# Another order of the first norm and the token mixer, and an output projection that ends with the prompt's tile and picks the prompt's tokens by one-hot products

## The chip, the cores and the metric

The program runs on one core of one Trainium2 chip. The metric is the device time of one execution in microseconds (us); lower is better. A core has five instruction queues that run beside each other, each strictly in its own order: TensorE (PE) for products, VectorE (DVE), ScalarE (ACT) and GpSimd (POOL) for elementwise work, and SyncE (SP), which here issues nearly all loads and stores. An instruction starts when it is first in its queue and what it waits for on the other engines has come.

## The reference, cut to what matters

One layer is computed for a prompt of 128 tokens (context) and 1024 latent tokens, with model width 1024: a modulated norm, a token mixer, a gated residual, a second modulated norm, and 16 experts that choose their tokens.

```python
mod = silu(c) @ w_mod + b_mod                    # 6 rows of 1024, once for the prompt, once for the latents
hn  = rmsnorm(x, norm1) * (1 + scale1) + shift1
u   = hn @ w_in                                  # p (512), v (1024), g1 and g2 (1024 each)
v   = conv4(v);  r, i = sigmoid(v @ w_r), sigmoid(v @ w_i)
a   = exp(-8 * r * softplus(-lam));  h_t = a h + sqrt(1 - a*a) * i * v      # scanned both ways
merged = sigmoid(g1) * (pool(p) @ w_br_pool) + sigmoid(g2) * (y_lru @ w_br_lru)
x  = x + gate1 * (merged @ w_out)
hn = rmsnorm(x, norm2) * (1 + scale2) + shift2
aff = softmax(hn @ router_w);  gate, idx = top_k(aff per expert, 2 * n / 16)   # 16 prompt, 128 latent tokens
out = (silu(hn[idx] @ w1) * (hn[idx] @ w3)) @ w2 * gate                        # for each of 16 experts
x  = x + gate2 * scatter_add(out);  y = rmsnorm(x, final)
```

## The kernel before

The 1152 tokens lie in tiles of 128: tile 0 is the prompt, tiles 1 to 8 the latents. A product in near fp32 precision is made of three passes: each weight block is loaded as `raw`, ScalarE rounds it to `hi` (L188), VectorE takes the rest as `lo` (L189), and PE adds hi·x_hi, hi·x_lo and lo·x_hi (L198 to L200). `do_split(n)` issues loads and splits for all entries of a list of work, `seq`, below n; it runs some four entries ahead of the products. There are three `raw` buffers, each free again once its `lo` is made.

The stages follow each other: the first norm with the modulation rows it needs (entries `a`; chunks in `DP` go through PE unsplit) to about 85 us; the mixer to about 565 us; the branch projection (L757) to about 665 us; the output projection (L984 to L986, two halves of 512 columns a tile, in the order of `steps`) to 803.3 us; a transition to the first expert product (L1465) at 832.6 us; then 16 experts of some 79 us each.

In the mixer each entry of `seq` is a block of 128 output channels: `v`, `g2`, `g1`, `p`, `bp`. Between them stand entries `m`, each eight products for a part of the remaining modulation rows (L665, L666). For each block j of v, `gates(j)` makes four groups of products and four Sigmoids on ScalarE (L527), `gates_rest(j)` is a row of Tanh, Exp, Square and Sqrt on ScalarE (L537 to L547) alternating with VectorE (L543 to L548), and `scans(j)` is VectorE's scan and what follows it (L559 to L568). [...] At ("g1", 0) the code runs `scans(6)`, `gates(7)`, then the splits of the next entries, and leaves `gates_rest(7)` in the list `rests` until the next `m` is done; then ("g2", 7) follows.

In the projection `project(i, h)` multiplies the sum by the gate row (`tmp`, L980) and adds it to the tile's x (L981), both on VectorE. `norm2` of a finished tile stores x (`x3_d`) and hn (`hn_d`, for the prompt `hp_d`) from SP. The router's products, the softmax (`affinities`), and the ranks among the latents (`first_rank`, `part_ranks`, a comparison with a transposed row) are hung into later steps; `prompt_a`, `prompt_b`, `prompt_c` choose the prompt's 16 tokens for each expert. Tile 8 comes last, so its norm, router and rank stand in the transition, followed by the latent list (`list_make`), an indirect gather of the first expert's rows from `hn_d` on POOL's queue (L1315), transposes of what it brought (L1446), and the first expert. `gate2_to` gives out 16 products of the last modulation row (L1299) in between, on w_mod blocks loaded into `hi` tiles by SP (L1292). Experts' weights come in 1 MB chunks (L1268).

Of the kernel before, what the change touches and what calls it, by code (L numbers as in the profile page):

```python
# [49 lines left out]
def hybrid_step_kernel(ctx: ExitStack, tc: tile.TileContext, x_prompt, x_sample, state_lru, c, c_ctx,  # L50
# [23 lines left out]
    hp_d = dram.tile([SP, D], F32, name="hp_d")  # L74
# [46 lines left out]
    l_a = ini.tile([P, 16], F32, name="l_a")  # L121
    l_e = ini.tile([P, 16], F32, name="l_e")
    l_z = ini.tile([P, 16], F32, name="l_z")
    l_q = ini.tile([P, 16], F32, name="l_q")
# [105 lines left out]
    for n, jb in enumerate(seq[4:]):  # L230
        full.append(jb)
        if n < 32 - 2 * NGT:
            full.append(("m", n))
# [118 lines left out]
    def hn_cols(k):  # L352
        for x, z in ((xv[:, k, 0, :SP], 0), (xv[:, k, 0, SP:], 1), (xv[:, k, 1:], 1)):
            V.tensor_scalar(x, x, s1[:, z, k:k + 1], modc[:, 0, z, k:k + 1], op0=OP.mult, op1=OP.add)
        A.copy(hn_hi[:, k, :].rearrange("p (g t) -> p g t", g=3), xv[:, k])
# [88 lines left out]
    hn_first(0)  # L444
    do_split(8)

    for q in range(4):
        k = 2 * q
        if q < 3:
            do_split(4 * q + 10)  # L450
# [3 lines left out]
        hn_cols(k + 1)  # L454
# [4 lines left out]
        if q < 3:  # L459
            mod_low(q + 1)  # L460
            do_split(4 * q + 12 if q < 2 else HEAD + 2)
# [6 lines left out]
    softplus()  # L468
# [19 lines left out]
    LR = {}  # L488

# [119 lines left out]
    def pool_evac(g, a3):  # L609
# [95 lines left out]
    rests = []  # L705
    load_gates(0)
    v_evac(va[0])
    conv(0)
    for j in range(2):
# [12 lines left out]
    for i in range(HEAD + 2, len(seq)):  # L722
        kind, j = seq[i]
        if kind == "m" and (kind, j) not in spl and i < done_split[0]:
            continue
        if (kind, j) != ("g1", 0):
            do_split(i + 4)
        for d in list(later):
            d[0] -= 1
            if d[0] <= 0:  # L730
                d[1]()
                later.remove(d)
        if kind == "bl" and j == 0:
            mg_hi = pool_sb["dp"].tile([P, KD, T], F32R, name="mg_hi", tag="D")
            mg_lo = big.tile([P, KD, T], F32R, name="mg_lo", tag="H2")
        if kind == "m":
            mod_block(j // 2, j % 2, spl.pop((kind, j)))
            for f in rests:
                f()
            rests = []  # L740
# [137 lines left out]
    g1r, mrows = [wo_g[:, KD * D:(KD + 1) * D].bitcast(F32), wop.tile([P, D], F32, name="g1r1")], {}  # L878
    for z in range(2):
        G.dma_start(g1r[z], row(z))  # L880
    x2s = {}
    for i in (1, 2):
        x2s[i] = sgp.tile([P, T], F32, name="sg")[:, :D]
        G.dma_start(x2s[i], x_rows(i))
# [9 lines left out]
    pgi = route.tile([P, 2], I32, name="pgi")  # L894
# [44 lines left out]
    def load_mrows(z):  # L939
        mrows[z] = [tk.tile([P, D], F32, name=f"s2r{z}", bufs=1),  # L940
                    tk.tile([P, D], F32, name="t2r", bufs=1) if z else rk.tile([P, D], F32, name="t2r0", tag="arow")]
        for n in range(2):
            SY.dma_start(mrows[z][n], row(2 + 2 * n + z))

    SY.dma_start(x2p, x_rows(0))
    load_mrows(1)
    load_mrows(0)

    def last_rows():
        x2s[8] = tk.tile([P, D], F32, name="x2l", tag="s2r0", bufs=1)  # L950
        SY.dma_start(x2s[8], x_rows(8))
# [3 lines left out]
    def project(i, h, mid=(), part=False):  # L955
        z = 1 if i else 0
        hs = slice(h * 512, (h + 1) * 512)
        if h == 0 and i not in x2s:
            x2s[i] = x2p if i == 0 else sgp.tile([P, T], F32, name="sg")[:, :D]
            if i:  # L960
                SY.dma_start(x2s[i], x_rows(i))
# [19 lines left out]
        V.tensor_tensor(x2s[i][:, hs], x2s[i][:, hs], tmp, op=OP.add)  # L981
# [12 lines left out]
    def norm2_b(i, n=1):  # L994
        z = 1 if i else 0
        x2, hn = x2s[i], hns[i]
        for q in range(n):
            s = slice(q * D // n, (q + 1) * D // n)
            V.scalar_tensor_tensor(hn[:, s], x2[:, s], rs2[:, i:i + 1], mrows[z][0][:, s], op0=OP.mult, op1=OP.mult)
            V.tensor_tensor(hn[:, s], hn[:, s], mrows[z][1][:, s], op=OP.add)  # L1000
        if z:
            SY.dma_start(x3_d[(i - 1) * P:i * P, :], x2)
        SY.dma_start(hn_d[(i - 1) * P:i * P, :] if i else hp_d[:, :], hn)
# [6 lines left out]
    def router_a(i):  # L1010
        hts[i] = tk.tile([P, KD, P], F32, name="ht", bufs=1)
        for h in range(2):
            t = tp_tile()
            for k in range(4):
                PE.transpose(t[:, k * P:(k + 1) * P], x2s[i][:, (4 * h + k) * P:(4 * h + k + 1) * P], ident)
            A.copy(hts[i][:, 4 * h:4 * h + 4, :], t.rearrange("p (a b) -> p a b", a=4))

    def router_b(i):
        z = 1 if i else 0
        t = tp_tile()  # L1020
        for k in range(KD):
            PE.matmul(t[:, :E], hts[i][:, k, :], rws[:, z, k, :], start=k == 0, stop=k == KD - 1)
        lts[i] = t
# [71 lines left out]
    def last_rank():  # L1095

        beat = first_rank(7, 0, 8, 1)
        t = tp_tile()
        for i in range(7):
            PE.matmul(t[:, i:i + 1], beat[:, i * P:(i + 1) * P], ones[:, 0:1], start=True, stop=True)  # L1100
        V.tensor_reduce(rank, wins, axis=AX.X, op=OP.add)
        V.tensor_tensor(rank[:, :7], rank[:, :7], t[:, :7], op=OP.subtract)

# [84 lines left out]
    def prompt_c():  # L1188
# [7 lines left out]
        V.tensor_copy(pgi, pgf)  # L1196
# [6 lines left out]
    steps = [(1, 0), (0, 0), (1, 1), (0, 1)] + [(i, h) for i in range(2, NT) for h in range(2)]  # L1203

    pre, mids, post = ([[] for _ in steps] for _ in range(3))
    n = 4
    for i in [1, 0] + list(range(2, NT - 1)):
        n = max(n + 1, 2 * i + 2)
        a, b = (4, KD - 1)
        mids[n].append((a, lambda i=i: router_a(i)))  # L1210
        mids[n].append((b, lambda i=i: (router_b(i), router_c(i))))
    pre[2].append(constants)
    pre[8].append(last_rows)
    pre[2].append(router_weights)
    mids[4].append((KD - 1, router_shift))
# [581 lines left out]
```

## Time and profile before

| | us |
|---|---|
| median of 3 runs | 2151.72 (2150.81 to 2152.35) |
| profiled execution | 2155.95 |
| its span, first to last instruction | 2154.2 |
| PE busy in the span | 2070.4 (96%) |
| DVE, ACT, POOL busy | 1709.6, 1358.8, 190.9 |

The span is what the trace covers; 1.75 us of the profiled execution lie around it. An engine's busy time says how full it was over all stages; what a change is worth in one stage is read from what PE waits for there. The granted clock of PE is 0.983 in the mean: in a few stretches it is half.

### The profile page before, as it was taken

Reading aid. Unit: us, or ns where it says so; the run is one execution under the profiler, and the core shown is the slowest. Engines: PE = TensorE matmul, PEld = TensorE weight load, DVE = VectorE, ACT = ScalarE, POOL = GpSimd, SP = SyncE. Lnnn points to the kernel's source line nnn. Section 1 sums busy time; section 2 is a strip of 40 time slices with the busy share of each in tenths; the row PEclk is TensorE's granted clock in tenths of the full one; section 3 lists DMA queues with packets and bytes.
Section 4 is the critical chain, followed back from the end, with each engine's and each line's share of the span. In section 5 each row is a group of like instructions: output and inputs, shape, how many; then the busy total and the mean of one; then the engine's idle time right before and its main releaser. Section 6 shows DMA issues by size and latency. Waiting matters only on the chain.

```text
span 2154.2 us, 40533 instructions
## 1 busy us (share of the span) xinstructions
PE 2070.4 (96%) x17269; PEld 1974.4 (92%) x17269; DVE 1709.6 (79%) x1847; ACT 1358.8 (63%) x1444; POOL 190.9 (9%) x324
## 2 busy tenths in 40 slices
PE   6999999999999987899999999999999999999995
PEld 4799998999998875899999999999999999999994
DVE  6788988732236467988988898998998998899896
ACT  6477675321112225677877777877877777777783
POOL 0000001010101001020010010011010011011021
PEclk9999999999999988999999999999999999999997
DMA  8133434174644238699999999999999999999995
GB/s 265 56 118 114 125 111 124 55 223 117 203 158 170 109 110 296 237 326 332 346 328 334 343 331 324 343 340 326 333 335 327 338 341 328 336 341 323 339 313 181
DMA packets 304820, 543.91 MB, mean 252 GB/s; under 512 B 16300, under 2 KB 85628, under 8 KB 304639
## 3 DMA queue, kind: packets, MB, share of 16 engines
q1 hardware_dynamic: 285306, 478.56, 64.0%
q0 software_dynamic: 15728, 52.77, 8.4%
q10 hardware_dynamic: 3604, 9.98, 1.4%
q8 instruction: 135, 2.21, 0.4%
q14 instruction: 47, 0.38, 0.1%
HBM read 500.60 MB, written 40.67 MB: 251 GB/s over the span
## 4 chain that ended last, share of the span: by engine, by line
PE 86%; DVE 8%; DMA 2%; ACT 2%; issue 1%; SPq 0%; DVEq 0%; ACTq 0%
PE ac L1465 37%; PE ac L1473 17%; PE a L198 6%; PE a L199 6%; PE a L200 6%; PE a L757 5%; DVE lo L1280 2%; PE a L984 1%; PE a L986 1%; PE a L985 1%; DMA xg<-hn_d,lgi 1%; PE tp L1404 1%; PE tp L1489 1%; DVE lo L189 1%; PE tp L665 1%
## 5 line engine op out<-in xcount | busy, mean ns | idle before, releaser
L1280 DVE TENSOR_TENSOR lo<-raw,hi 128x2048 bf16<-128x2048 f32 x384 | 870.9, 2281 | 0.0
L1274 ACT CAST hi<-raw 128x2048 fp32r<-128x2048 f32 x384 | 729.4, 1912 | 3.8 <-issue 2.2
L1465 PE MATMUL ac<-x,hi 128*128 128x288 f32 x4096 | 606.1, 300 | 0.0
L1465 PEld LDWEIGHTS ac<-x,hi 128*128 128x128 f32 x4096 | 553.0, 189 | 1.0 <-issue 0.9
L1473 PEld LDWEIGHTS <-lo 128*128 128x128 bf16 x6144 | 380.4, 98 | 36.7 <-DVE lo L1280 0.8
L1465 PE MATMUL ac<-hh,hi 128*128 128x288 f32 x2048 | 332.9, 304 | 0.0
L1478 ACT COPY bs<-ac 128x288 f32<-128x288 f32 x320 | 127.8, 399 | 290.6 <-PE ac L1473 289.1
L1473 PE MATMUL ac<-xb,lo 128*128 128x144 bf16 x4096 | 302.4, 227 | 0.6 <-DVE lo L1280 0.6
L1465 PEld LDWEIGHTS ac<-hh,hi 128*128 128x128 f32 x2048 | 279.9, 189 | 0.0
L198 PE MATMUL a<-hn_hi,hi 128*128 128x384 f32 x624 | 212.0, 340 | 0.0
L199 PE MATMUL a<-hn_lo,hi 128*128 128x384 f32 x624 | 210.8, 338 | 0.0
L200 PE MATMUL a<-hn_hi,lo 128*128 128x384 f32 x624 | 210.8, 338 | 0.0
L1473 PE MATMUL ac<-hb,lo 128*128 128x144 bf16 x2048 | 171.9, 227 | 0.0
L189 DVE TENSOR_TENSOR lo<-raw,hi 128x1024 fp32r<-128x1024 f32 (+1 forms) x76 | 86.7, 1163 | 78.8 <-ACT hi L188 78.2
L1479 DVE TENSOR_TENSOR h<-ac,bs 128x288 f32<-128x288 f32 x256 | 115.7, 452 | 42.1 <-ACT bs L1478 41.8
L198 PEld LDWEIGHTS a<-hn_hi,hi 128*128 128x128 f32 x624 | 117.1, 188 | 0.4
L199 PEld LDWEIGHTS a<-hn_lo,hi 128*128 128x128 f32 x624 | 117.2, 188 | 0.0
L200 PEld LDWEIGHTS a<-hn_hi,lo 128*128 128x128 f32 x624 | 117.2, 188 | 0.0
L1710 POOL TENSOR_TENSOR yps<-ot,modc 128x128 f32<-128x128 f32 x16 | 35.9, 2247 | 735.2 <-DVE ot L1479 735.2
L188 ACT CAST hi<-raw 128x1024 fp32r<-128x1024 f32 (+1 forms) x76 | 74.8, 1001 | 41.2 <-PE a L199 33.3
L1479 DVE TENSOR_TENSOR ot<-ac,bs 128x288 f32<-128x288 f32 x64 | 29.3, 457 | 69.7 <-ACT bs L1478 69.7
L699 ACT ACTIVATE sg<-a 128x1152 f32<-128x1152 f32 x16 | 18.1, 1134 | 82.4 <-PE a L200 82.3
(447 smaller groups left out, 2626.8 us busy)
## 6 DMA issues: line engine op xcount, KB each, us to landing
raw<-in_exp_w_dram SPq DMA_DIRECT2D x380, 1024.0 KB, 7.2
raw<-in_w_in_dram SPq DMA_DIRECT2D x28, 512.0 KB, 5.0
raw<-in_w_mod_dram SPq DMA_DIRECT2D x28, 512.0 KB, 5.3
araw<-in_w_mod_dram SPq DMA_DIRECT2D x18, 256.0 KB, 4.5
g_d<-sg ACTq DMA_DIRECT2D x8, 576.0 KB, 3.2
yh_d<-yh POOLq DMA_DIRECT2D x8, 576.0 KB, 3.1
yl_d<-yl POOLq DMA_DIRECT2D x8, 576.0 KB, 4.6
m_d<-sg POOLq DMA_DIRECT2D x8, 576.0 KB, 4.2
```

Source lines behind the costliest of these rows:

```text
L188: A.copy(h, raw)
L189: V.tensor_tensor(l, raw, h.bitcast(F32), op=OP.subtract)
L198: PE.matmul(out, whi, xhi, start=first, stop=False)
L199: PE.matmul(out, whi, xlo, start=False, stop=False)
L200: PE.matmul(out, wlo, xhi, start=False, stop=last)
L757: PE.matmul(a3[:, ch, :CH], w[:, k, :], y[:, k, cs], start=n == 0 and k == 0 and w is hi, stop=n == 1 and k == KD - 1 and w is ws[-1])
L1274: A.copy(hl[n][0], raw[n])
L1280: V.tensor_tensor(lo, r, hi.bitcast(F32), op=OP.subtract)
L1465: PE.matmul(a[:, r, :2 * S], w[0][:, k, c0 + r * P:c0 + (r + 1) * P], x2(kk), start=kk == first, stop=False)
L1473: PE.matmul(a[:, r, S:2 * S], w[1][:, k, c0 + r * P:c0 + (r + 1) * P], xb(kk), start=False, stop=kk == last)
L1478: A.copy(b, a[:, :, S:2 * S])
L1479: V.tensor_tensor(dst, a[:, :, :S], b, op=OP.add)
```

## The change

Seven things are altered, in two regions.

First norm and mixer. Three chunks of modulation weights instead of four go unsplit. Some splits of the head stand earlier, `hn_cols` is cut in its VectorE part (`hn_mod`, now ahead of the splits' `lo`) and its ScalarE part, the copy of `mrow1` is one instruction of ScalarE, and the 21 small instructions of `softplus` stand behind `conv(0)`. In `seq`, four `m` follow ("g1", 0) instead of one, and fewer stand later. A new function `sums_next(n)` runs the next n entries `m`: one behind each `v_evac` and inside each `pool_evac`, four at ("g1", 0) between `scans(6)` and `gates(7)`. `gates_rest(7)` is issued at once, behind `gates(7)`.

Projection and transition. The latents come first and tile 0 last, so that norm, router and rank of tile 8 run under tile 0's products. The addition into x of tiles 1 to 7 goes to POOL. The prompt's choice comes after the loop. The two gathers of prompt rows from `hp_d` go; in their place `prompt_pick` builds a one-hot matrix (scaled by the norm), and `prompt_cols` multiplies x of the prompt by it, eight products of 128x128 for each half of the experts, and applies scale and shift as it copies. `gate2_to` gives eight products in the transition and eight behind the first group of expert 0 (only the last two of four column blocks are made here). All five first expert chunks are issued by SP, two ahead of the w_mod blocks; ScalarE issued four (chunks 2 to 5) before.

```diff
-DP = range(4)
+DP = range(3)
...
     for jb in seq[4:]:
         full.append(jb)
-        if n < 32 - 2 * NGT:
-            full.append(("m", n))
+        for _ in range(4 if jb == ("g1", 0) else 1):
+            if n < 32 - 2 * NGT:
+                full.append(("m", n))
+                n += 1
...
+            hn_mod(k + 1)
+        do_split(4 * q + 10 if q < 3 else HEAD + 2)
         dense_v(0, k)
...
-        hn_cols(k + 1)
+        hn_high(k + 1)
         dense_v(1, k)
...
+    def sums_next(n):
+
+        while n and seq[at[0] + 1][0] == "m":
+            at[0] += 1
+            m = seq[at[0]][1]
+            do_split(at[0] + 1)
+            turn_later()
+            mod_block(m // 2, m % 2, spl.pop(("m", m)))
...
             if j == 0:
                 g1s[j] = gate_evac(a3)
                 scans(KD - 2)
+                sums_next(4)
                 gates(KD - 1)
                 do_split(i + 5)
-                rests.append(lambda: gates_rest(KD - 1))
+                gates_rest(KD - 1)
...
-        V.tensor_tensor(x2s[i][:, hs], x2s[i][:, hs], tmp, op=OP.add)
+        (G if 0 < i < NT - 1 else V).tensor_tensor(x2s[i][:, hs], x2s[i][:, hs], tmp, op=OP.add)
...
-    steps = [(1, 0), (0, 0), (1, 1), (0, 1)] + [(i, h) for i in range(2, NT) for h in range(2)]
+    steps = [(1, 0), (2, 0), (1, 1), (2, 1)] + [(i, h) for i in list(range(3, NT)) + [0] for h in range(2)]
...
-    load_chunk(0)
+    for n in range(2):
+        load_chunk(n)
     for j in range(4 - NGT, 4):
-        if j == 5 - NGT:
-            SY.dma_start(x3_d[7 * P:, :], x2s[8])
         gate2.append(ew.tile([P, 8, 256], F32R, name="hi", bufs=HB).bitcast(F32))
...
     xg = x_fetch(hn_d[:, :], lgi[:, 0:1])
-    ahead(1, 0)
+    for n in range(2, RB):
+        load_chunk(n)
+    affinities(0, 1)
+    prompt_a()
+    gate2_to(1)
+    prompt_b()
+    gate2_to(8)
+    prompt_c()
...
+        V.tensor_scalar(oh, iof, pgf[:, g:g + 1], None, op0=OP.is_equal)
+        t = tp_tile()
+        PE.transpose(t[:, :P], oh, ident)
+        A.activation(pick, t[:, :P], AF.Copy, scale=rs2[:, 0:1])
...
+                PE.matmul(t[:, k * P:(k + 1) * P], x2p[:, (4 * h + k) * P:(4 * h + k + 1) * P], pick,
+                          start=True, stop=True)
...
+    prompt_pick(0)
+    ahead(1, 0)
+    prompt_cols(0)
...
-        next(find)
-        ahead(2, 1)
...
+        ahead(2, 0)
+        for n in range(2):
+            load_chunk(RB + n)
+        next(find)
         ahead(4, 0)
```

In the programs' order, ScalarE around ("g1", 0) and ("g2", 7): before, from the Sigmoids of `gates(7)` (L527) to the gate of ("g2", 7) (`sg`, L699); `hi<-raw` is a split, L537 to L547 are `gates_rest(7)`.

```order
207 L527 ACTIVATE gate<-a_2867,col_a 128x1158
208 L188 CAST hi<-raw 128x1024 x2
209 L669 COPY mrow<-tp 4x256
210 L537 ACTIVATE lt<-gate,pk 128x1158 x2
211 L540 ACT_TABLE_LOAD
212 L540 ACTIVATE gate<-gate,nk 128x1158
213 L542 ACTIVATE lq<-gate 128x1158
214 L540 ACTIVATE gate<-gate,nk 128x1158
215 L542 ACTIVATE lq<-gate 128x1158
216 L547 ACT_TABLE_LOAD
217 L547 ACTIVATE lt<-lt 128x1158 x2
218 L188 CAST hi<-raw 128x1024
```

ScalarE after, at the same place (the numbers of lines have moved by a few: L528 is the Sigmoid, L182 the split, L538 to L548 are `gates_rest(7)`, L701 is the gate of ("g2", 7)):

```order
209 L528 ACTIVATE gate<-a_2924,col_a 128x1158
210 L538 ACTIVATE lt<-gate,pk 128x1158 x2
211 L541 ACT_TABLE_LOAD
212 L541 ACTIVATE gate<-gate,nk 128x1158
213 L543 ACTIVATE lq<-gate 128x1158
214 L541 ACTIVATE gate<-gate,nk 128x1158
215 L543 ACTIVATE lq<-gate 128x1158
216 L548 ACT_TABLE_LOAD
217 L548 ACTIVATE lt<-lt 128x1158 x2
218 L182 CAST hi<-raw 128x1024 x4
219 L701 ACT_TABLE_LOAD
220 L701 ACTIVATE sg<-a_2978 128x1152
```

Between the last Sigmoid and Tanh two splits and an `mrow` copy stood before; now nothing does, and four splits, the first of them that of ("g2", 7), stand behind Sqrt.

VectorE in the same stretch before, from the end of `scans(6)` (L567, L568) over `gates_rest(7)` to the start of `scans(7)` (L559); L189 is the `lo` of a split.

```order
287 L567 CAST yh<-lt 128x1024
288 L568 TENSOR_TENSOR yl<-lt,yh 128x1024
289 L189 TENSOR_TENSOR lo<-raw,hi 128x1024 x2
290 L543 SCALAR_TENSOR_TENSOR lt<-lq,lt 128x1158 x2
291 L545 TENSOR_TENSOR gate<-gate,vc 128x1158 x2
292 L548 TENSOR_TENSOR gate<-gate,lt 128x1158 x2
293 L189 TENSOR_TENSOR lo<-raw,hi 128x1024
294 L559 SCALAR_TENSOR_TENSOR lt<-gate 128x128
```

VectorE after (L569 ends `scans(6)`, L211 and L212 place a modulation row, L183 is the `lo`):

```order
288 L569 TENSOR_TENSOR yl<-lt,yh 128x1024
289 L211 TENSOR_TENSOR mtmp<-tp,col_b 128x4
290 L212 TENSOR_TENSOR modc<-tp,mtmp 128x2x2
291 L183 TENSOR_TENSOR lo<-raw,hi 128x1024 x2
292 L544 SCALAR_TENSOR_TENSOR lt<-lq,lt 128x1158 x2
293 L546 TENSOR_TENSOR gate<-gate,vc 128x1158 x2
294 L549 TENSOR_TENSOR gate<-gate,lt 128x1158 x2
295 L183 TENSOR_TENSOR lo<-raw,hi 128x1024 x4
296 L560 SCALAR_TENSOR_TENSOR lt<-gate 128x128
```

The two `lo` behind `scans(6)` were for entries after ("g2", 7), and are now those of the last two of the four `m`; the `lo` of ("g2", 7) is now the first of the four behind `gates_rest(7)`.

SP's loads and stores in the transition before (`x_d` and `hn_d` are stores of tile 8, L1268 the expert chunks, L1292 the w_mod blocks):

```order
124 L1268 DMA raw<-in_exp_w_dram 128x4x512
125 L1292 DMA hi<-in_w_mod_dram 128x8x256
126 L1290 DMA x_d<-x2l 128x1024
127 L1292 DMA hi<-in_w_mod_dram 128x8x256
128 L1344 DMA hn_d<-hn 128x1024
129 L1268 DMA raw<-in_exp_w_dram 128x4x512 x4
```

SP after:

```order
120 L1007 DMA x_d<-sg 128x1024
121 L1008 DMA hn_d<-hn 128x1024
122 L1302 DMA raw<-in_exp_w_dram 128x4x512 x2
123 L1325 DMA hi<-in_w_mod_dram 128x8x256 x2
124 L1302 DMA raw<-in_exp_w_dram 128x4x512 x9
125 L1622 DMA rows_d<-ot 1x512
```

Two expert chunks now stand ahead of the w_mod blocks, and the stores of tile 8 ahead of all of them.

## Rows read from the trace of the kernel before

**Rows 1.** The page's first lines: span; busy time, share, instructions of PE.

```profile
span 2154.2 us, 40533 instructions
PE 2070.4 (96%) x17269; PEld 1974.4 (92%) x17269; DVE 1709.6 (79%) x1847; ACT 1358.8 (63%) x1444; POOL 190.9 (9%) x324
```

**Rows 2.** PE's timeline, mixer: start us, us, instruction, idle before and its releaser.

```profile
324.12 0.61 PE L198 MATMUL a<-vhi,ghi 128*128 128x386 f32 x1 [2.63 <-ACT sg L699]
...
332.08 0.28 PE L665 MATMUL tp<-hi,cond 128*128 128x256 f32 x1
...
333.02 0.35 PE L198 MATMUL a<-hn_hi,hi 128*128 128x384 f32 x1
```

**Rows 3.** ACT's timeline, mixer: last Sigmoid of gates(7), splits, gates_rest(7), next split.

```profile
332.34 1.23 ACT L527 ACTIVATE gate<-a,col_a 128x1158 f32<-128x1158 f32 x1 [0.42 <-PE a L200]
333.46 1.98 ACT L188 CAST hi<-raw 128x1024 fp32r<-128x1024 f32 x2
...
335.61 2.41 ACT L537 ACTIVATE lt<-gate,pk 128x1158 f32<-128x1158 f32 x2
...
347.92 1.04 ACT L188 CAST hi<-raw 128x1024 fp32r<-128x1024 f32 x1
```

**Rows 4.** DVE's timeline, mixer: first and last of scans(6), and splits behind.

```profile
324.76 0.41 DVE L559 TENSOR_TENSOR_SCAN lt<-gate 128x128 f32<-128x128 f32 x1
...
332.82 1.23 DVE L568 TENSOR_TENSOR yl<-lt,yh 128x1024 fp32r<-128x1024 f32 x1
334.53 2.36 DVE L189 TENSOR_TENSOR lo<-raw,hi 128x1024 fp32r<-128x1024 f32 x2 [0.48 <-ACT hi L188]
...
350.89 1.22 DVE L189 TENSOR_TENSOR lo<-raw,hi 128x1024 fp32r<-128x1024 f32 x1
```

**Rows 5.** Windows: stretch, length, busy of PE, PEld, DVE, ACT, POOL, clock, DMA share, GB/s.

```profile
34.10:40.90 6.80, 5.69 (x15) 3.36 (x16) 6.38 (x9) 6.17 (x8) 0.00 (x0) 0.50 0.51 159
320.00:330.00 10.00, 5.87 (x25) 5.05 (x24) 9.97 (x12) 6.38 (x6) 0.00 (x0) 0.83 0.00 1
771.40:778.20 6.80, 4.36 (x12) 3.09 (x11) 2.79 (x7) 0.23 (x1) 0.00 (x0) 0.75 0.43 154
778.20:791.90 13.70, 12.70 (x35) 10.18 (x36) 7.38 (x29) 2.81 (x4) 2.28 (x5) 0.50 0.10 39
803.30:832.60 29.30, 17.16 (x92) 8.75 (x90) 18.55 (x52) 12.46 (x21) 11.38 (x11) 0.77 0.84 297
```

**Rows 6.** PE's waits from 27 to 86 us, in total, times, longest.

```profile
PE a L198 <- ACT hn_hi L362: 4.1, 3, 2.7
PE a L199 <- DVE hn_lo L368: 2.6, 4, 1.0
```

**Rows 7.** PE's waits from 664 to 834 us.

```profile
PE tp L1092 <- DVE cols L1081: 3.4, 1, 3.4
```

**Rows 8.** Lines of VectorE, 664 to 804 us: count, busy, mean ns, idle before.

```profile
L981 DVE TENSOR_TENSOR sg<-sg,tmp 128x512 f32<-128x512 f32 x14 | 9.7, 692 | 13.6 <-issue 9.7 <-DMA sg<-in_x_sample_dram 3.6
```

**Rows 9.** POOL's timeline in the transition.

```profile
809.88 2.48 POOL L1343 TENSOR_TENSOR hn<-hn,t2r 128x512 f32<-128x512 f32 x2 [0.25 <-ACT hn L1331]
```

**Rows 10.** DVE's timeline beside it.

```profile
810.41 0.77 DVE L1044 TENSOR_TENSOR lg<-lg,mx 128x16 f32<-128x16 f32 x1
```

**Rows 11.** DMA issues from 785 to 835 us: count, KB, median us to landing.

```profile
raw<-in_exp_w_dram ACTq DMA_DIRECT2D x4, 1024.0 KB, 11.1
...
hi<-in_w_mod_dram SPq DMA_DIRECT2D x2, 1024.0 KB, 5.2
...
xg<-hn_d,lgi POOLq DMA_INDIRECT x1, 10.1
```

**Rows 12.** PE's timeline at the end of the transition.

```profile
829.81 1.94 PE L1446 MATMUL tp<-ident,xg 128*128 128x128 f32 x8 [7.26 <-DMA xg<-hn_d,lgi]
...
832.62 0.61 PE L1465 MATMUL ac<-x,hi 128*128 128x288 f32 x2
```

**Rows 13.** PE's waits from 832 to 934 us, in expert 0.

```profile
PE tp L1374 <- DVE msk L1367: 10.3, 6, 2.5
```

More of the change, by code (lines that the diff above doesn't have):

```diff
@@ L432, in hybrid_step_kernel @@
     x_cols1(1, 1, A)
+    do_split(4)
     mod_first(0)
@@ L444, in hybrid_step_kernel @@
     hn_first(0)
+    hn_mod(1)
     do_split(8)
@@ L459, in hybrid_step_kernel @@
         if q < 3:
+            do_split(min(4 * q + 12, HEAD))
             mod_low(q + 1)
-            do_split(4 * q + 12 if q < 2 else HEAD + 2)
         dense_v(0, k + 1)
@@ L488, in hybrid_step_kernel @@
     LR = {}
+    l_a, l_e, l_z, l_q = (lp.tile([P, 16], F32, name=f"l{n}") for n in "aezq")
     def load_gates(j):
@@ L708, in hybrid_step_kernel @@
     conv(0)
+    softplus()
     for j in range(2):
@@ L721, in hybrid_step_kernel, with turn_later @@
             scans(0)
[L722 to L727, printed above, removed]
+    def turn_later():
         for d in list(later):
@@ L732, in hybrid_step_kernel @@
                 later.remove(d)
+    def sums_next(n):
[5 more added lines that the diff above has]
+            mod_block(m // 2, m % 2, spl.pop(("m", m)))
+            if m == 31 - 2 * NGT:
+                later.append([5, mod_rows])
+            n -= 1
+    at = [HEAD + 1]
+    while at[0] + 1 < len(seq):
+        at[0] += 1
+        i = at[0]
+        kind, j = seq[i]
+        if (kind, j) != ("g1", 0):
+            do_split(i + 4)
+        if kind == "m":
+            turn_later()
         if kind == "bl" and j == 0:
@@ L937, in router_shift @@
         A.copy(lsh, t[:, :2 * E].rearrange("p (z e) -> p z e", z=2))
[L939 to L943, printed above, removed]
-    SY.dma_start(x2p, x_rows(0))
[L946 to L951, printed above, removed]
+    x2s[2] = tk.tile([P, D], F32, name="x2e", bufs=1)
+    SY.dma_start(x2s[2], x_rows(2))
+    mrows = []
+    for n in range(2):
+        mrows.append(tk.tile([P, D], F32, name=f"mr{n}", bufs=1))
+        SY.dma_start(mrows[n], row(3 + 2 * n))
+    SY.dma_start(x2p, x_rows(0))
     pss = {}
@@ L1008, in norm2, with router_a, router_b @@
         norm2_b(i)
[L1010 to L1018, printed above, removed]
+    def router_a(i, h):
+        if h == 0:
+            hts[i] = tk.tile([P, KD, P], F32, name="ht", bufs=1)
+        t = tp_tile()
+        for k in range(4):
+            PE.transpose(t[:, k * P:(k + 1) * P], x2s[i][:, (4 * h + k) * P:(4 * h + k + 1) * P], ident)
+        A.copy(hts[i][:, 4 * h:4 * h + 4, :], t.rearrange("p (a b) -> p a b", a=4))
+    def router_b(i, ks=range(KD)):
         z = 1 if i else 0
[L1020 to L1023, printed above, removed]
+        if i not in lts:
+            lts[i] = tp_tile() if i else acc2.tile([P, 512], F32, name="a2")
+        for k in ks:
+            PE.matmul(lts[i][:, :E], hts[i][:, k, :], rws[:, z, k, :], start=k == 0, stop=k == KD - 1)
     def router_c(i):
@@ L1435, in parts_of @@
             return lambda: A.copy(xb[:, ks, a:b], x)
-        parts_of(xps[0][:, :, :PCAP], slice(0, KD), CAP, S, G)()
-        for n in range(2, RB + 2):
-            load_chunk(n, A if n <= RB else SY)
-        next(find)
-        ahead(2, 1)
+        parts_of(xps[0][:, :, :PCAP], slice(0, KD), CAP, S, V)()
         low = []
```

215 lines of the change are left out of this document (101 added, 114 removed).

## The prediction

> **What bounds the kernel now.** The page's first lines say that PE is busy for 96% of the span [rows 1], so only what PE waits for, and stretches in which it runs at half clock, can be won or lost. I therefore read PE's waits stage by stage, and for each wait the queue of the engine it names. Five places matter. In the head, from 27 to 86 us, PE waits 4.1 us for `hn_hi` and 2.6 us for `hn_lo` [rows 6], and from 34.1 to 40.9 us the granted clock is 0.50 [rows 5], that is 1.2 instead of 2.4 GHz. In the mixer around ("g1", 0) PE waits 2.63 us [rows 2], the largest share of what stands in 320 to 330 us [rows 5]; otherwise it runs through. In the projection it waits 3.4 us for `cols` [rows 7], and the clock is half for part of 771.4 to 778.2 and all of 778.2 to 791.9 us [rows 5]. The transition is 29.3 us [rows 5] and ends with 7.26 us for the gather [rows 12]. In expert 0 PE waits 10.3 us for VectorE's search of the prompt's and latents' thresholds [rows 13]. The experts after it are full of PE and the change leaves their products as they are.
>
> **The mixer, first place: four m between scans(6) and gates(7).** Before, `gates(7)` follows the gate of ("g1", 0) at once and its four groups are through at 332.08 us, where an `m` begins; the `m` takes 0.94 us, and ("g2", 7) starts at 333.02 us [rows 2]. Now the four `m` must be through first. Two of them are split ahead; the splits of the last two have their `lo` on VectorE behind `scans(6)`, as the order shows. `scans(6)` runs from 324.76 to 334.05 us [rows 4], since it waits for `gates_rest(6)`, which the change does not move. What stands behind it is the two `lo`, 2.36 us together [rows 4], 1.2 each. So the third `m` starts at about 335.3 and ends at 336.2 us. The order puts the fourth `hi` on ScalarE behind the copy of the row that the third ends: about 1.2 us with the copy (half of the pair at 333.46 is 1.0, [rows 3]), then a `lo` of 1.2, then 0.94 for the `m`: about 339.6 us. `gates(7)` is four groups; three took 332.08 minus 324.12, less one short wait, some 6.3 us, so four take 8.4 [rows 2]. It ends at 348.0 instead of 332.08 us, 15.9 later. Three `m` of 0.94 are only brought forward, so 2.8 come back later: **+13.1 us**. Ends: +9 if scans and their gates come out earlier, since all of the mixer starts earlier by the head's gain; +18 if the last `raw` load, which waits for a buffer that a `lo` frees, adds 5 us (a 1 MB load took 5.2, [rows 11]).
>
> **The mixer, second place: the split of ("g2", 7) behind gates_rest(7).** Before, PE began ("g2", 7) at 333.02 us [rows 2] and the splits issued there came later, at 333.46 [rows 3]: it had been split long before, and ran under `gates_rest(7)`. Now `do_split(i + 5)` counts from ("g1", 0), and with four `m` behind it reaches only them. The order has the `hi` of ("g2", 7) behind Sqrt on ScalarE and its `lo` behind the last product of gates on VectorE. PE has nothing else in its queue there. The cost is what lies between the end of `gates(7)` on PE and that `lo`: 1.5 us to the end of the last Sigmoid (332.34 + 1.23 - 332.08), then the stretch from Tanh at 335.61 to the `lo` at 350.89 + 1.22, which is 16.5 us [rows 3, 4]; less 0.35 for two products that need no `lo`: **+17.6 us**. ScalarE alone gives the lower end: Tanh to the next `hi` is 335.61 to 347.92, and that `hi` takes 1.04, so 14.8 with the Sigmoid [rows 3]. No other work can cover it, so the upper end is 18.
>
> **The clock behind these waits.** After a wait of 2.63 us the clock of 320 to 330 us is 0.83 in the mean [rows 5], and in the head, where the longest wait is 2.7 us [rows 6], it is 0.50 for 6.8 us [rows 5]. Two waits of over 10 us should each be followed by a stretch at half clock. At 0.50, 6.8 us hold 3.4 us of work, so each costs 0 to 3.4 us; before, one such stretch of half that length is paid for already. I take **+4 us** for both, with ends 0 and 7.
>
> **The head.** A fourth chunk split instead of direct adds a `hi` and a `lo` (1.04 and 1.22, [rows 3, 4]), and PE takes four cheaper products for two dear ones. `hn_mod` ahead of the `lo` of the splits is aimed at the 4.1 and 2.6 us of [rows 6]. Some of these waits stay, as the same VectorE makes modulation, splits and `hn_lo`, in another order. I take 4 of the 6.7 us: **-4 us**, ends 0 and -8 (all of it and a little of the half clock). `softplus` behind `conv(0)` moves some 5 us of small instructions to where VectorE is off the path: 0, and +2 if `gates_rest(0)` waits for it.
>
> **Projection.** The 3.4 us wait [rows 7] and half clock over 13.7 us plus half of 6.8 us [rows 5] are together up to 12 us. Their source is not the prompt's tile but SP's order: VectorE's addition stood idle for loads of x, in total 3.6 us by releaser and 9.7 without one [rows 8], since each load is issued behind the stores of an earlier tile. That stays. POOL takes 14 additions of 0.692 us [rows 8] off VectorE, and does each in 1.24 [rows 9], so each norm comes 0.55 us later for each half. New transposes of tile 8 and 0 sit between the products. I take **-1 us**, ends -12 and +10 (14 times 0.692, if the additions end up in VectorE's way).
> While POOL ran two such additions, a VectorE instruction on 128x16, whose neighbours take some 0.2 us, took 0.77 [rows 9, 10]. The Trainium skill, GPSIMD Engine Reference, section 8 (Key points), says that GpSimd shares its SBUF interfaces with VectorE and contends with instructions of two SBUF inputs; the trace agrees. By that rule each of the 14 additions can hold up VectorE once, and this speaks against the change; it is the rival below.
>
> **Transition.** Its critical path is now the w_mod block, not the gather. Before, each block landed 5.2 us after its issue; four expert chunks issued together took 11.1 us each [rows 11]. Now two chunks and two blocks are issued together when the projection's buffers come free, so the first block comes 11 us after some 1 us. Then follow, in PE's order: 8 products of gate2 (1.9, like the 8 transposes), the prompt's choice and `prompt_pick` (3 us of handing over, my estimate), 8 one-hot products of the transposes' shape (1.94), their copies (1.1), and the transposes up to the first expert product, 829.81 to 832.62, 2.8 us [rows 12]. The sum is 22.7 against 29.3 [rows 5]: -6.6. The gather (10.1, [rows 11]) lands under it. But in expert 0, which the search limits [rows 13], 8 products of gate2 (2 us) and the splits of chunk 1 (twice the columns of the mixer's, so twice 1.04 and 1.22 us, [rows 3, 4]), which formerly ran under the gather, now come after, and the search starts behind them: +7. Together **0 us**, ends -9 and +9. At expert 7 eight one-hot products stand for eight transposes: 0.
>
> **The sum.** 13.1 + 17.6 + 4 - 4 - 1 + 0 = +29.7 us. On the profiled 2155.95 that is 2185.7. That execution lies 4.2 us over the median of 2151.72, so the median should be 2181.4; I say **2181 us**.
>
> **The rivals.** *POOL in VectorE's way:* if each of 14 additions holds up VectorE by its own 1.24 us, norms and ranks come later by up to 17 us; if two thirds of it reach PE, through `cols` (my estimate), that is +12, 2193 us. For it: the 0.77 [rows 10]; against: VectorE has slack under the products. *Half the mixer's loss:* if the first place costs nothing, because the last two `m` are split before the scans block VectorE, and projection and head give their -12 and -6, the result is 17.6 + 2 - 6 - 12 + 0 = +2 to +8, 2154 to 2160 us. *The other side, faster:* the tail as the bound. If the projection gives its full 12, the transition its 9 without loss in expert 0, and the head 8, they give 29 and outweigh the mixer as soon as its two places cost less than that; with the first place at nothing and 17.6 + 2 for the second the time is 2151.7 - 9, 2142 us. For it: waits and half clock of that size do stand in the rows [rows 5 to 7, 12]. Against: both places in the mixer follow from queue order, and nothing in PE's queue covers them. *The change does not do what it says:* the scheduler could have put the split elsewhere; the order shows it has not.
>
> **How the numbers follow.** Forecast 0.63 (2170 to 2196 us from the ends of the large terms), POOL 0.14, half the loss 0.11, faster 0.12. Leaving out the last and the tail above 2200, some 0.17 in all, the range is 2154 to 2200 us. What a measurement can tell from no change is about 0.2%, 4.3 us. Faster by more than that is the last rival, 0.12; within it falls a part of half the loss, 0.05; slower 0.83.
>
> **What would show it.** In the trace after: a wait of PE on ScalarE's or VectorE's split ahead of ("g2", 7), 13 to 18 us long; waits of some 10 us in sum for `m` ahead of `gates(7)`; a half clock behind each; the first dense product of the branch projection later by some 25 to 30 us. In the head fewer waits for `hn_lo`; in the transition a wait for the w_mod `hi` of 5 to 9 us in place of the gather's 7.26. If PE starts ("g2", 7) without a wait, the forecast is wrong.

## The result and the profile after

The changed kernel takes 2183.9 us in the median (2183.42 to 2185.29) beside 2151.84: 1.0153 times the time before, with a 95% interval of 1.0139 to 1.0168. It is 1.5% slower. The profiled execution took 2185.29 us, its span is 2183.4.

The page's first lines after, which answer to [rows 1]: PE is busy 3 us longer in a span that is 29.2 us longer, so most of the loss is waiting. What half clock costs is hidden in the busy time, and shows stage by stage.

```profile
span 2183.4 us, 40571 instructions
PE 2073.4 (95%) x17287; PEld 1978.9 (91%) x17287; DVE 1704.3 (78%) x1849; ACT 1363.2 (62%) x1453; POOL 197.7 (9%) x331
```

Where the 29.2 us lie is seen from the start of the first product of each stage in the two traces (us):

| stage | before | after | change | on record |
|---|---|---|---|---|
| to the first dense block behind the head | 85.7 | 82.6 | -3.1 | -4 |
| from there through the mixer, to the branch projection | 479.5 | 511.2 | +31.7 | +34.7 |
| branch projection | 101.5 | 101.4 | -0.1 | 0 |
| output projection, first to last product | 136.2 | 126.8 | -9.4 | -1 |
| transition, to the first expert product | 29.7 | 30.7 | +1.0 | -6.6 |
| expert 0 | 103.0 | 106.8 | +3.8 | +7 |
| expert 7 | 79.5 | 85.7 | +6.2 | 0 |
| all else, rounding among it | | | -0.9 | -0.4 |
| sum | | | +29.2 | +29.7 |

The mixer in windows, before and after (stretch, length, busy of PE, PEld, DVE, ACT, POOL, clock, DMA share, GB/s):

```profile
85.70:565.20 479.50, 471.98 (x2740) 466.88 (x2738) 325.60 (x358) 249.97 (x261) 22.72 (x97) 1.00 0.41 121
82.60:593.80 511.20, 478.19 (x2740) 470.99 (x2739) 328.06 (x378) 250.31 (x262) 22.73 (x97) 0.96 0.38 114
```

The same 2740 instructions of PE are busy 6.2 us longer, at a lower mean clock, and PE waits 25.5 us longer (33.0 instead of 7.5).

PE's waits from 300 to 370 us after (in total, times, longest), where before there were 6.2 us (2.6 [rows 2] and 1.5 at the gates, 2.1 for `modc`) and no wait for a split:

```profile
PE a L192 <- ACT hi L182: 14.6, 1, 14.6
PE tp L668 <- DVE lo L183: 9.3, 2, 8.6
PE tp L667 <- ACT mrow L671: 3.5, 1, 3.5
PE a L194 <- DVE lo L183: 2.2, 1, 2.2
PE tp L667 <- ACT hi L182: 1.4, 1, 1.4
```

The second, third and last of these are the `m` ahead of `gates(7)`, the first and fourth are ("g2", 7). ScalarE's timeline shows what the 14.6 us wait stands behind. It answers to [rows 3].

```profile
346.41 1.23 ACT L528 ACTIVATE gate<-a,col_a 128x1158 f32<-128x1158 f32 x1 [0.43 <-PE a L194]
347.54 2.40 ACT L538 ACTIVATE lt<-gate,pk 128x1158 f32<-128x1158 f32 x2
...
357.68 2.23 ACT L548 ACTIVATE lt<-lt 128x1158 f32<-128x1158 f32 x2
359.81 2.92 ACT L182 CAST hi<-raw 128x1024 fp32r<-128x1024 f32 x3
```

From the first Tanh at 347.54 to the first `hi` at 359.81 nothing on ScalarE is for PE. VectorE's timeline shows the other place, which answers to [rows 4]:

```profile
329.63 1.23 DVE L569 TENSOR_TENSOR yl<-lt,yh 128x1024 fp32r<-128x1024 f32 x1
...
331.04 1.23 DVE L183 TENSOR_TENSOR lo<-raw,hi 128x1024 fp32r<-128x1024 f32 x1
335.56 1.23 DVE L183 TENSOR_TENSOR lo<-raw,hi 128x1024 fp32r<-128x1024 f32 x1 [3.29 <-ACT hi L182]
```

L569 ends `scans(6)`. Right behind it (and two short instructions for a modulation row) comes the `lo` that PE stood 8.6 us for; the second `lo` is delayed by the `hi` that ScalarE makes behind the copy of the third m's row. Windows of the same stretch (columns as above) show PE's share of it, and the clock:

```profile
320.00:330.00 10.00, 2.29 (x9) 1.99 (x9) 9.86 (x14) 2.31 (x3) 0.11 (x1) 0.54 0.00 1
330.00:340.00 10.00, 5.60 (x20) 5.02 (x21) 3.46 (x5) 1.31 (x2) 0.96 (x2) 0.50 0.69 222
340.00:350.00 10.00, 6.32 (x32) 5.90 (x31) 0.00 (x0) 7.25 (x7) 0.00 (x0) 0.93 0.01 2
350.00:360.00 10.00, 0.00 (x0) 0.00 (x0) 4.97 (x4) 9.59 (x9) 0.00 (x0) 0.58 0.00 0
360.00:370.00 10.00, 6.95 (x24) 6.45 (x25) 7.18 (x7) 4.71 (x5) 0.00 (x0) 0.57 0.44 131
```

In 320 to 330 us [rows 5] has 5.87 us of PE, here it is 2.29. The clock is at half where PE has been idle, and stays there for a while when products come again.

The head's waits from 27 to 86 us answer to [rows 6]: 4.1 us for `hn_hi` became 1.7, 2.6 for `hn_lo` became 1.9, and the clock from 34.1 to 40.9 us rose from 0.50 to 0.75. Behind the later of these waits it falls, though: from 40.9 to 86 us it is 0.96, and was 1.00 before.

```profile
PE a L193 <- DVE hn_lo L367: 1.9, 1, 1.9
PE a L192 <- ACT hn_hi L361: 1.7, 1, 1.7
```

The transition on PE's timeline, which answers to [rows 12]:

```profile
828.30 0.38 PE L1180 MATMUL tp<-ident,lg 128*16 128x128 f32 x1 [1.60 <-DVE lg L1049]
835.59 5.62 PE L1332 MATMUL ac<-hi,sil 128*4 128x256 f32 x16 [6.91 <-DMA hi<-in_w_mod_dram]
841.14 1.05 PE L1202 MATMUL tp<-one,pblk 16*128 16x1 f32 x8
843.13 0.30 PE L1372 MATMUL tp<-ident,oh 128*128 128x128 f32 x1 [0.94 <-DVE oh L1370]
843.88 2.05 PE L1380 MATMUL tp<-pick,x2p 128*128 128x128 f32 x16 [0.46 <-ACT pick L1373]
849.75 1.00 PE L1473 MATMUL tp<-ident,xg 128*128 128x128 f32 x4 [3.81 <-ACT xp L1386]
```

L1332 are the gate2 products, L1202 the last step of the prompt's choice, L1380 the one-hot products, L1473 the transposes of the gathered rows. The gate2 products wait 6.91 us for their weights, and everything of the prompt stands behind them in PE's queue.

In expert 7, where PE had no wait before, it has one:

```profile
1468.40 0.48 PE L1372 MATMUL tp<-ident,oh 128*128 128x128 f32 x1 [3.67 <-DVE oh L1370]
```

### The profile page after: what moved, and what is told of

Same layout as the page of the kernel before. It is cut to its first block, busy times and chain, and to the rows that moved or that the text cites. A ratio compares the mean times of both kernels' runs of the same rounds, so it can differ in the third digit from the quotient of the medians.

```text
span 2183.4 us, 40571 instructions
## 1 busy us (share of the span) xinstructions
PE 2073.4 (95%) x17287; PEld 1978.9 (91%) x17287; DVE 1704.3 (78%) x1849; ACT 1363.2 (62%) x1453; POOL 197.7 (9%) x331
## 4 chain that ended last, share of the span: by engine, by line
PE 86%; DVE 9%; ACT 2%; DMA 2%; issue 1%; SPq 0%; POOL 0%; DVEq 0%; ACTq 0%; POOLq 0%
PE ac L1493 36%; PE ac L1501 17%; PE a L193 6%; PE a L194 6%; PE a L192 6%; PE a L774 5%; DVE lo L1314 2%; PE a L993 1%; PE a L995 1%; PE a L994 1%; PE tp L667 1%; PE tp L668 1%; PE tp L1441 1%; PE tp L1517 1%; DMA hi<-in_w_mod_dram 1%
## 5 line engine op out<-in xcount | busy, mean ns | idle before, releaser
L192 PE MATMUL a<-hn_hi,hi 128*128 128x384 f32 x624 | 212.2, 340 | 14.6 <-ACT hi L182 14.6
L183 DVE TENSOR_TENSOR lo<-raw,hi 128x1024 fp32r<-128x1024 f32 (+1 forms) x77 | 88.0, 1165 | 71.7 <-ACT hi L182 71.7
L182 ACT CAST hi<-raw 128x1024 fp32r<-128x1024 f32 (+1 forms) x77 | 76.0, 1002 | 40.4 <-PE a L193 24.5
L701 ACT ACTIVATE sg<-a 128x1152 f32<-128x1152 f32 x16 | 18.2, 1135 | 92.3 <-PE a L194 92.2
```

The costliest lines, as they stand in the source:

```text
L182: A.copy(h, raw)
L183: V.tensor_tensor(l, raw, h.bitcast(F32), op=OP.subtract)
L192: PE.matmul(out, whi, xhi, start=first, stop=False)
```

## The experiments

Each is compared with runs of the kernel before on the same chip; those medians were 2151.95, 2153.63 and 2151.99 us in the three groups of runs. The changed kernel's 2183.9 is from the first measurement. Stage times are taken as in the table above. The end of the head differs from execution to execution: 82.6 us in the trace above, 79.9 to 82.3 in the ten traces below that have the changed head. So what a run changes in the mixer is read from the mixer alone, from the first dense block to the branch projection of the same trace.

**The split of ("g2", 7) ahead of gates_rest(7).** To the changed kernel:

```diff
                 gates(KD - 1)
-                do_split(i + 5)
+                do_split(at[0] + 2)
                 gates_rest(KD - 1)
```

> Changed kernel, but the split of (g2,7) is issued ahead of gates_rest(7). My theory: this removes only the second place in the mixer, PE's 14.6 + 2.2 us wait for that split and the half clock behind it, about 19 us: 2165 us. Rival (the stretch is bound by gates_rest and scans, not by the order of one split): the wait moves to the next block and less than 6 us come back, 2178 us or more.

Measured: 2172.26 us, ratio 1.0098 (1.0082 to 1.0115); 11.6 us come back, of 19 expected. The mixer alone is 11.1 us shorter (500.1 instead of 511.2), so all of it is there. Rows of PE's timeline with a wait, of this run:

```profile
347.44 0.44 PE L192 MATMUL a<-hn_hi,hi 128*128 128x384 f32 x1 [2.31 <-ACT hi L182]
348.69 0.45 PE L194 MATMUL a<-hn_hi,lo 128*128 128x384 f32 x1 [0.64 <-DVE lo L183]
363.84 0.47 PE L668 MATMUL tp<-lo,cond 128*128 128x256 f32 x1 [2.06 <-DVE lo L183]
```

16.8 us of waiting became 5.0. The `hi` still stands behind the last Sigmoid of `gates(7)`, and the next `m`, which is split behind `gates_rest(7)`, takes over 2.06 us. The order of this split is the cause. The rival came in part as well: with the split one entry ahead of its products, 5.0 us of waiting remain, and some of it has moved to the next block.

**The last two m split ahead of scans(6).**

```diff
                 g1s[j] = gate_evac(a3)
+                do_split(i + 5)
                 scans(KD - 2)
```

> Changed kernel, but the last two of the four m are split ahead of scans(6). My theory: this removes only the first place, the waits of 3.5, 9.3 and 1.4 us ahead of gates(7) with their half clock, 14 to 17 us: about 2168 us. Rival: ScalarE, which is late with gates_rest(6), makes PE wait at the acc buffers instead, and under 8 us come back: 2176 us or more.

Measured: 2173.72 us, ratio 1.0106 (1.0089 to 1.0123): 10.2 us less than the changed kernel. The mixer alone is 11.2 us shorter (500.0 instead of 511.2). The branch projection begins at 580.0 us, 13.8 earlier, of which 2.7 are the head's; expert 7 takes 1.4 us more in the profiled execution. The 14.2 us of waiting for `m` became 5.8, and all of it is now for the copy of the row on ScalarE. The 14.6 us at ("g2", 7) stay untouched:

```profile
PE a L192 <- ACT hi L182: 14.6, 1, 14.6
PE tp L667 <- ACT mrow L671: 5.8, 2, 5.3
```

**Both splits ahead, four m kept.** The two edits above in one kernel.

> Changed kernel with four m, the last two of them split ahead of scans(6) and (g2,7) split ahead of gates_rest(7). My theory: the two places add, 11.6 + 10.2 us come back, 2162 us, and what is left over the run with one m (2157 us) is the wait for the copy of the row in front of the third m. Rival: with both splits ahead, the waits join behind ScalarE, and less than 18 us come back: 2166 us or more.

Measured: 2160.3 us, ratio 1.004 (1.0025 to 1.0054). 23.6 us come back, against 11.6 + 10.2 for the two alone, and the mixer alone is 23.6 us shorter (487.6), against 11.1 + 11.2: they add, within what such runs can tell. The wait of 5.8 us for the row's copy remains, as expected.

**One m behind ("g1", 0).**

```diff
-        for _ in range(4 if jb == ("g1", 0) else 1):
+        for _ in range(1):
```

> Changed kernel with one m behind (g1,0) instead of four; nothing else is undone. My theory: both places in the mixer are due to the count of four alone, so the mixer is as long as in the kernel before and 31.7 us come back: 2152 us, the same as before. Rival: the other new places of the m (inside pool_evac, ahead of gates) cost something of their own: 2158 us or more.

Measured: 2157.16 us, ratio 1.0027 (1.0017 to 1.0038). 26.7 us come back of 31.7 expected. In the profiled execution the mixer alone takes 482.3 us, 28.9 less than in the changed kernel and 2.8 more than before; 1.7 of these 2.8 are more waiting of PE in the mixer (10.1 us in sum against 8.4). Its span of 2154.2 is the same as before's, though the medians differ by 5.2 us: profiled executions lie above the median by 4.2 us before [as in the table ahead of the prediction] and below it by 0.8 here. The runs of the kernel before differ with their granted clock: in this group the fastest took 2148.32 us at 0.986 and the slowest 2155.64 at 0.983, and the profiled one, at 0.983, is of the slow end. The count of four is the cause of nearly all of the mixer's loss; what else is new there (the other places of `m`, `gates_rest(7)` at once) costs up to 2.8 us in this trace, and was not separated.

**All additions into x on VectorE.**

```diff
-        (G if 0 < i < NT - 1 else V).tensor_tensor(x2s[i][:, hs], x2s[i][:, hs], tmp, op=OP.add)
+        V.tensor_tensor(x2s[i][:, hs], x2s[i][:, hs], tmp, op=OP.add)
```

> Changed kernel with all additions of the projection into x on VectorE, as before. My theory after the trace: the projection's gain of 9.3 us comes from the new order of tiles, not from POOL, so this run is within 3 us of the changed kernel (2181 to 2187). Rival A: POOL's relief carries the gain, then 2190 us or more. Rival B, the one on record, POOL in VectorE's way: then 2178 us or less.

Measured: 2191.66 us, ratio 1.019 (1.0173 to 1.0207), 7.8 us more than the changed kernel. The projection takes 134.2 instead of 126.8 us. My theory fell: the new order of tiles gives 2.0 us (136.2 to 134.2), POOL 7.4. PE's wait is back, at the same place as in [rows 7] (waits from 695 to 830 us), and VectorE's timeline says why:

```profile
PE tp L1097 <- DVE cols L1086: 4.6, 1, 4.6
```

```profile
790.85 0.69 DVE L990 TENSOR_TENSOR sg<-sg,tmp 128x512 f32<-128x512 f32 x1 [3.64 <-DMA sg<-in_x_sample_dram]
791.46 0.18 DVE L1041 TENSOR_REDUCE mx<-lg 128x2 f32<-128x32 f32 x1
```

The addition of tile 7 stands first in VectorE's queue and waits for its x. Behind it stands the softmax of earlier tiles, for which PE waits.

**The kernel before with the additions on POOL, and nothing else.**

```diff
-        V.tensor_tensor(x2s[i][:, hs], x2s[i][:, hs], tmp, op=OP.add)
+        (G if 0 < i < NT - 1 else V).tensor_tensor(x2s[i][:, hs], x2s[i][:, hs], tmp, op=OP.add)
```

> Kernel before with one thing of the change: the additions into x of tiles 1 to 7 on POOL. My theory: VectorE's relief is what shortened the projection by 7 of 9.3 us, so this run is 5 to 8 us faster than before, 2145 us. Rival: with the prompt's tile second and the old routers the stall hangs on the load of x behind SP's stores, and the gain is under 2 us, 2150 us or more; POOL's 1.29 us instead of 0.69 per addition could even cost 2.

Measured: 2141.57 us, ratio 0.9946 (0.9933 to 0.9959): 12.1 us faster than before. The projection takes 124.0 us instead of 136.2, and less than the 126.8 of the changed kernel: with the additions on POOL the new order of tiles, with the 14 instructions of PE that it brings into the projection, costs 2.8 us. The kernel before's 666 instructions of PE in the projection are busy 124.0 us instead of 132.0, so of the 12.2 us 8.0 were half clock and 4.2 waiting. PE has no wait from 664 to 792 us, and the clock, which in [rows 5] fell to 0.75 and 0.50 from 771.4 us on, holds (windows; columns as above):

```profile
765.00:778.00 13.00, 13.00 (x75) 11.02 (x75) 9.68 (x37) 4.20 (x8) 1.29 (x2) 1.00 0.33 122
778.00:790.60 12.60, 12.60 (x70) 10.75 (x69) 8.87 (x30) 6.59 (x10) 3.53 (x6) 1.00 0.43 152
```

In the kernel before VectorE's queue stood at the same addition, of tile 7, with `cols` behind it:

```profile
776.81 0.69 DVE L981 TENSOR_TENSOR sg<-sg,tmp 128x512 f32<-128x512 f32 x1 [3.68 <-issue]
...
778.76 0.29 DVE L1081 COPY cols<-lg 128x256 f32<-128x256 f32 x1
```

No releaser is named for the 3.68 us, but SP issued that tile's load at 772.84 us, and these loads took 3.9 us in the median to land.

The line of POOL's additions, 664 to 791 us (count, busy, mean ns, idle before and releasers), is the answer to [rows 8]:

```profile
L981 POOL TENSOR_TENSOR sg<-sg,tmp 128x512 f32<-128x512 f32 x14 | 18.0, 1290 | 84.1 <-DMA sg<-in_x_sample_dram 50.4 <-DVE tmp L980 33.7
```

The loads of x come about as late as before (that of tile 7 was issued at 770.69 us): POOL stands 50.4 us for them. But on POOL nothing is queued behind the wait.

**The gate2 products behind the one-hot products.**

```diff
     prompt_a()
-    gate2_to(1)
     prompt_b()
-    gate2_to(8)
     prompt_c()
...
     ahead(1, 0)
     prompt_cols(0)
+    gate2_to(8)
```

> Changed kernel, but the first eight gate2 products stand behind the one-hot products instead of ahead of the prompt's choice. My theory: the 6.9 us wait for the w_mod block lay on the path in front of the whole prompt chain; now that chain runs under the load, and the first expert product comes 6 to 8 us earlier: about 2177 us. Rival: the chunk loads, the first split and the copies that alternate between ScalarE and VectorE bind as well, and less than 3 us come back: 2181 us or more.

Measured: 2177.08 us, ratio 1.0112 (1.0095 to 1.0128), 6.8 us less than the changed kernel, as expected. The transition takes 22.7 instead of 30.7 us. On PE's timeline the wait for the weights is gone, and the gate2 products fill the wait for the copies of `xp` that had been 3.81 us:

```profile
830.79 1.83 PE L1202 MATMUL tp<-one,pblk 16*128 16x1 f32 x8 [2.61 <-DVE pblk L1194]
...
834.46 3.78 PE L1378 MATMUL tp<-pick,x2p 128*128 128x128 f32 x16 [0.46 <-ACT pick L1371]
838.17 3.94 PE L1332 MATMUL ac<-hi,sil 128*4 128x256 f32 x16
```

**The one-hot matrix of expert 7 one block earlier.** Its VectorE instruction is issued at block 1, PE transposes it at block 2 as in the changed kernel.

```diff
+                if e == 7 and (fb, w) == (1, 0):
+                    prompt_hot(1)
                 if e == 7 and (fb, w) == (2, 0):
                     prompt_pick(1)
```

> Changed kernel, but VectorE makes the one-hot matrix of experts 8 to 15 one block of expert 7 earlier than PE transposes it. My theory: the 6 us that expert 7 gained are the 3.7 us wait of PE behind VectorE's queue and the half clock after it; about 5 us come back: 2179 us. Rival: the products themselves (16 fp32 passes for 8 transposes) are the cost, and under 2 us come back: 2182 us or more.

Measured: 2179.21 us, ratio 1.0122 (1.0106 to 1.0138), 4.7 us less. Expert 7 takes 80.5 us instead of 85.7 (before: 79.5), and PE has no wait from 1400 to 1520 us. So of its 6.2 us 5.2 were the wait of 3.67 us and the half clock behind it, and 1.0 the products.

**The changed kernel with three repairs:** one `m`, gate2 products late, one-hot matrix early.

> Changed kernel with one m behind (g1,0), the gate2 products behind the one-hot products, and the one-hot matrix of expert 7 made early. If the gains add: 2157 - 7 - 5 = 2145 us. If the transition is bound elsewhere, 2150 us or more, no better than the kernel before.

Measured: 2142.91 us, ratio 0.9954 (0.994 to 0.9968). The gains add: 41.0 us less than the changed kernel, against 38.2 for the three alone. Transition and expert 0 together are 128.0 us, 4.7 less than before's 132.7; the projection is 126.9.

**The same, with the last gate2 products spread over the search of expert 0.**

```diff
-                             (lambda r: None if r == 0 else next(find, None)) if e == 0 and (fb, w, q) not in SKIP else None)
+                             (lambda r: None if r == 0 else (gate2_to(min(NGT * KD, gdone[0] + 1)), next(find, None))) if e == 0 and (fb, w, q) not in SKIP else None)
...
-                if (e, fb, w) == (0, 0, 0):
+                if (e, fb, w) == (0, 1, 0):
```

> The combination of before (one m, gate2 products behind the one-hot products, one-hot matrix of expert 7 early), and the last eight gate2 products given out one by one ahead of the steps of the search in expert 0, where PE waits for VectorE. My theory: their 3.7 us go under waits of 5.9 us, 2 to 4 us come back: about 2140 us. Rival: they delay the transposes that VectorE's search waits for, and nothing comes back.

Measured: 2142.56 us, ratio 0.9958 (0.9945 to 0.9971): no change. Expert 0 is 105.0 us in both. PE's wait for the search (`msk`, 830 to 870 us) fell from 5.9 to 4.9 us only. The rival's outcome came, but whether by its mechanism was not measured apart.

**The kernel before with two parts of the change: additions on POOL, and the head.** The head's part is that of the diff ahead of the prediction (`DP`, earlier splits, `hn_mod` and `hn_high`, one copy of the row, `softplus` behind `conv(0)`).

> Kernel before with two things of the change: the additions of tiles 1 to 7 on POOL, and the new order of the first norm with softplus behind conv(0). My theory: both gains add, 2141.6 less the 3.1 us that the first dense block behind the head came earlier: 2138.5 us. Rival: the mixer's waits at its own gates take the head's gain back, 2141 us or more.

Measured: 2136.64 us, ratio 0.9931 (0.9917 to 0.9945): 15.4 us faster than the kernel before and 47 faster than the changed one, the best of all. The branch projection begins at 561.3 us instead of 565.0 with POOL alone.

## Why the prediction was right, and where its steps were not

The forecast of 2181 us lies 2.9 us below the 2183.9 measured, and the sum of +29.7 us beside +29.2. The mechanism that carried it, two places in the mixer, is what the runs show. The signs on record came as well, only the waits for `m`, put at some 10 us, were 14.2. But four other terms were off, and the errors nearly cancel: the projection's 8.4 us against the transition's 7.6, and expert 7's 6.2 against the mixer's 3.0 and expert 0's 3.2. The precision of the sum is luck.

- *The mixer, +34.7 on record with the clock, +31.7 measured.* Both places are where the order put them. The wait at ("g2", 7) is 16.8 us against 17.6. `gates(7)` ends at 346.2 us, or 17.2 later than before if the head's 3.1 us are set aside, against 15.9. The experiments separate the two places, 11.6 and 10.2 us, and the one-m run accounts for 28.9 of the 31.7 us in its trace. The clock's term, 4 us, is small: the 6.2 us more of busy time for the same instructions are what half clock cost, within the ends of 0 and 7. Two readings were wrong without much harm: before, PE did not run through beside the 2.63 us, but waited 1.5 us more at the same gates and 2.1 us for `modc`; and the stretch from which 8.4 us for `gates(7)` were taken ran in part at half clock (it took 7.7).
- *The head, -4 on record, -3.1 measured.* Right in kind: the wait for `hn_hi` fell by 2.4 us, that for `hn_lo` by 0.7. In the ten other traces with this head it ends 3.4 to 5.8 us earlier than before. In the kernel before with POOL's additions it is worth 3.7 us at the branch projection (565.0 to 561.3), and 3.3 in the medians, each taken against its own group (12.1 and 15.4). Which of the head's parts does it was not separated.
- *The projection, -1 on record, -9.4 measured.* The step that failed is "VectorE's addition stood idle for loads of x [...] That stays." The loads did stay late; the wait did not stay in VectorE's queue. I had priced the additions by their duration, 14 times 0.692 against 14 times 1.24, and not by what stood behind the waiting addition: the softmax and `cols`, for which PE waited 3.4 us and lost its clock. The term itself was named ("together up to 12 us", with -12 as an end), and was held not to be won. The runs with the additions on VectorE and on POOL in both kernels show it: 7.4 and 12.2 us.
- *The rival of POOL in VectorE's way* had the wrong sign for the projection. Its mechanism is in the trace, but rare: in the kernel before with POOL's additions, of 15 VectorE instructions that ran at least 0.1 us beside one of them, 13 kept their duration. The other two are of L1114, which takes 0.35 us elsewhere; each ended 0.15 us behind POOL's addition:

```profile
758.96 1.29 POOL L981 TENSOR_TENSOR sg<-sg,tmp 128x512 f32<-128x512 f32 x1 [9.59 <-DMA sg<-in_x_sample_dram]
759.36 1.04 DVE L1114 SCALAR_TENSOR_TENSOR beat<-arow,lg,tri 128x128 bf16<-128x128 f32 x1
```

```profile
778.15 1.29 POOL L981 TENSOR_TENSOR sg<-sg,tmp 128x512 f32<-128x512 f32 x1 [2.17 <-DVE tmp L980]
779.17 0.42 DVE L1114 SCALAR_TENSOR_TENSOR beat<-arow,lg,tri 128x128 bf16<-128x128 f32 x1
```

  That is about 0.8 us on VectorE, and none of it reached PE, which has no wait there. The norm's two long instructions on 128x1024 never ran beside an addition, so the trace does not say what that would cost.
- *The transition, -6.6 on record, +1.0 measured.* The path was named rightly (PE's wait for the w_mod block is 6.91 us), and three of its pieces fit: 13.5 us to the block's landing against 12, 2.05 for the one-hot products against 1.94, 3.0 for the end against 2.8. The second of these is luck: each one-hot product is two passes (x16) at full clock here, and the eight transposes it was priced by ran at half clock; at full clock eight of them take 1.04 us in expert 7. Two were mis-sized. The gate2 products took 5.62 us instead of 1.9, a term I had priced by transposes: each is two passes, and the clock over these 5.6 us is 0.63. The wait for the copies was 3.8 instead of 1.1. Half of it is a split's `lo` ahead of them in VectorE's queue, the other half four copies of 0.4 us that ScalarE and VectorE make in turn:

```profile
845.65 2.29 DVE L1314 TENSOR_TENSOR lo<-raw,hi 128x2048 bf16<-128x2048 f32 x1 [2.67 <-ACT hi L1308]
847.86 0.41 DVE L1388 TENSOR_SCALAR xp<-tp,modcol 128x128 f32<-128x128 f32 x1
848.30 0.46 ACT L1386 ACTIVATE xp<-tp,modcol 128x128 f32<-128x128 f32 x1 [2.68 <-DVE xp L1388]
```

- *Expert 0, +7 on record, +3.8 measured:* the eight gate2 products took 3.6 us in this trace. PE is busy 5.9 us longer (95.0 against 89.1), at a mean clock of 0.93 against 0.97, and waits 2.1 us less. The 4.5 us of splits that stood in the term were not measured apart.
- *Expert 7, 0 on record, +6.2 measured.* The step "eight one-hot products stand for eight transposes" forgot the instruction in front of them: `prompt_pick` puts a VectorE instruction behind a full queue and PE's transpose right behind it. The experiment gives 5.2 of it back.

## What to carry to other kernels

Price an instruction that is moved to another engine by what stands in the queue behind its wait, not by its own duration: here an addition twice as slow on an idle engine saved 12 us in the kernel before and 8 in the changed one. When one piece of work is placed between two others, count what a look-ahead by index still covers: four entries in front of one used up its whole look-ahead. And where PE needs what a fuller engine makes, issue that engine's part one block ahead of PE's.

## What the runs showed of the hardware

The additions of POOL took 1.29 us each, 1.9 times VectorE's 0.692. VectorE's L1114, with `arow` and `tri` as inputs, did not end before an addition beside which it had started: 1.04 and 0.42 us instead of 0.35, ending 0.15 us behind it both times. The Trainium skill, GPSIMD Engine Reference, section 8 (Key points), speaks of contention with VectorE's instructions of two SBUF inputs; these two agree. The price here is about 0.8 us of VectorE's time, against the 12.2 us that the move won.

A short wait costs more than itself: in expert 7 the run without the wait of 3.67 us is 5.2 us shorter; with it the granted clock is 0.91 over the 20 us around it, and the other traces with the same wait have 85.7 to 87.1 us:

```profile
1460.00:1480.00 20.00, 16.33 (x156) 15.78 (x155) 14.18 (x13) 12.92 (x17) 0.00 (x0) 0.91 0.82 297
```
